# mLSTM outputs: mask sums, weights times queries and pooled remainders move from GpSimd to VectorE

## The chip, the cores and the metric

One core of one Trainium2 chip. The metric is the device time of one execution in microseconds (us), the median of 3 runs. TensorE (PE) multiplies, VectorE (DVE), ScalarE (ACT) and GpSimd (POOL) do elementwise work, SyncE (SP) issues transfers; ScalarE issues some too.

## The reference

One block of a diffusion transformer on 2048 tokens of width 1024, with 256 context tokens, in float32. The input is normalised and modulated, projected by `w_in` to a pooled half (512), queries and keys (256 each, with a short convolution and silu), values (512), an output gate o (512) and 16 gate rows. The middle is an mLSTM with 4 heads (64 wide for queries and keys, 128 for values) in both directions, beside a windowed mean of the pooled half. Then:

```python
    s = jnp.einsum('bhjd,bhsd->bhjs', qc, kc) * jnp.exp(dmat - m[..., None])
    w_inter = jnp.exp(inter - m)
    num = jnp.einsum('bhjs,bhsv->bhjv', s, vc) + w_inter[..., None] * jnp.einsum('bhvd,bhjd->bhjv', c0, qc)
    den = jnp.sum(s, axis=-1) + w_inter * jnp.einsum('bhd,bhjd->bhj', n0, qc)
    h = num / jnp.maximum(jnp.abs(den), jnp.exp(-m))[..., None]
    ...
    hn = hm * lax.rsqrt(jnp.mean(hm * hm, axis=-1, keepdims=True) + EPS)      # mlstm_output
    ...
    mix_x = jnp.concatenate([pool_x, mlstm_output(hx_m, ox, head_norm[l])], axis=-1) @ w_out[l]
    x = x + g1 * mix_x
    x = x + g2 * swiglu(modulate(rmsnorm(x, norm2[l]), sh2, sc2), w_up[l], w_down[l])
```

and a last rmsnorm. `dmat` is masked: only earlier tokens (for the other direction, later ones) count.

## The kernel before

The kernel runs in stages. To about 475 us it forms modulation, context, the projections (block products in seven instead of eight parts, `unit`) and the states of the mLSTM at the edges of 16 chunks of 128 tokens; `w_out` is loaded, scaled and split until about 515. From 505 to 820 us the outputs are formed chunk by chunk (chunks 7 to 0, then 15 to 8), and after that the up and down products of the swiglu run to the end.

Float32 products with full precision are made of three: an operand is split into a rounded part (`mh`, by ScalarE) and a remainder (`mlo`, by `split`, L151), and high times high, high times low and low times high are summed (L1171 to L1173).

The loop over chunks (from L1200) has five parts in an iteration t. `ml_a` of chunk t+1 loads a row of decay sums into X (named `raw` in the trace, 1024 wide, from `s_R`, broadcast to 128 partitions, one of three buffers), queries `qd` and a row of weights `wb` (from `s_W`, one of two buffers); TensorE forms keys times queries (`pqk`, L1090, one PSUM bank); X gets the mask added (L1092), `wb` is multiplied with the queries (L1093), ScalarE takes eight exponentials of X (L1097), and VectorE multiplies X by `pqk` (L1099). `proj` of chunk t-2 multiplies the mixed chunk by `w_out` in 48 matmuls (two halves of 24), adds the residual (L1176), stores it (`s_x`) and scales it by its norm (L1184, with the power `xrs` by GpSimd at L143). `second_norm`, in every second iteration, turns two chunks (transposes L290), applies the modulation (L297, L299), makes block sums (L306) and stores 1.8 MB to `s_hb`. `ml_b` of chunk t makes the outputs of both directions (`po`, L1114 with X, L1120 with `wb`), their divisors `rr` (L1125 to L1127), the sum of directions (L1131, L1132) and the norm of each head (L141, the power `hrs` at L143 by GpSimd, L1136). `prep` of chunk t-1 loads the gate `so`, the pooled half `pmx` and the residual, splits `pmx` (L1152), turns the head outputs (transposes L1155), gates them (L1157) and splits that (`mlo<-so`).

Three things set the order. Each engine runs its queue in the order written, and an instruction that waits holds all behind it. That order isn't the program's: a scheduler puts the instructions of each engine in order by a timeline of its own before the program is built, so that a change of engine for one instruction moves others. And buffers bind: a load of `raw` for chunk t+3 starts when the outputs of chunk t have read their X, and PSUM has three banks for projections and turns together. `ml_a` runs far ahead of its `ml_b` in this order, up to three chunks.

Of the kernel before, what the change touches and what calls it, by code (L numbers as in the profile page):

```python
# [12 lines left out]
ALU = mybir.AluOpType  # L13
# [8 lines left out]
def tile_hybrid_block(ctx: ExitStack, tc: tile.TileContext, x, c, cx, c_ctx, w_ada, b_ada, norm1, w_in, conv_qk,  # L22
                      gate_bias, pool_w, pool_scale, head_norm, w_out, norm2, w_up, w_down, norm_f, out):
    nc = tc.nc
    P = 128
# [20 lines left out]
    def r32(ap):  # L46
        return ap.bitcast(F32)
# [98 lines left out]
    def split(src, hi, lo, eng_hi, eng_lo):  # L146
        if eng_hi is nc.scalar:
            nc.scalar.copy(hi, src)  # L148
        else:
            eng_hi.tensor_copy(hi, src)  # L150
        eng_lo.tensor_tensor(lo, src, r32(hi), op=ALU.subtract)  # L151
# [207 lines left out]
    with pool("adap", 4, "right") as ap_:  # L359
        xc, turned = None, None  # L360
        for g in range(4):
            ks = range(2 * g, 2 * g + 2)
            pm = tp.tile([P, 512], F32, name="tp")[0:4, :]
# [37 lines left out]
            def col(o):  # L401
# [3 lines left out]
                                    op=ALU.add)  # L405
# [432 lines left out]
    for half in range(2):  # L838
# [8 lines left out]
        if half == 0:  # L847
# [11 lines left out]
            with pool("gp", 1) as gp:  # L859
# [5 lines left out]
                mask = gat.rearrange("p c g -> p (c g)").rearrange("p (d j) -> p d j", d=2)  # L865
# [29 lines left out]
    def dma_kv(kp, sk, sv, cc, bufs, vp=None):  # L895
        kT = kp.tile([P, 2, P], F32, name="kT", bufs=bufs)
        nc.sync.dma_start(kT, sk[:, cc * P:(cc + 1) * P].rearrange("(t p) c -> p t c", p=P))
        vt = vp.tile([P, 4, 129], F32, name="vta", bufs=2) if vp else vtp.tile([P, 4, 129], F32, name="vt")
        nc.sync.dma_start(vt.rearrange("p h v -> p (h v)"), sv[cc * P:(cc + 1) * P, :])
        return kT, vt  # L900
# [170 lines left out]
    def ml_a(n, cc):  # L1071
        csl = slice(cc * P, (cc + 1) * P)
        kT, vt = dma_kv(m2, s_k, s_v, cc, 2)
        qb = qbd[n % 2]
        qd = ld2.tile([P, 4, P], F32, name="qd")
        sq_ = s_q[:, csl]
        for hh in range(2):
            hs = slice(hh * 64, hh * 64 + 64)
            nc.sync.dma_start(qb[hs, :, hh, :], sq_.rearrange("(a b p) c -> b p a c", a=2, b=2)[hh])
            nc.sync.dma_start(qd[hs], sq_.rearrange("(h p) c -> p h c", p=64))  # L1080
        X = rwp.tile([P, 2, 4, P], F32, name="raw")
        nc.sync.dma_start(X.rearrange("p d h j -> p (d h j)"),
                          s_R[cc:cc + 1].rearrange("o d h j -> o (d h j)").to_broadcast([P, 8 * P]))
        wb = ld2.tile([P, 4, P], F32, name="wb")
        for d in range(2):
            ml_last[0] = nc.sync.dma_start(wb[d * 64:d * 64 + 64].rearrange("p h j -> p (h j)"),
                              s_W[cc, d:d + 1].rearrange("o h j -> o (h j)").to_broadcast([64, 4 * P]))
        pqk = pqp.tile([P, 512], F32, name="pqk")
        for p_ in range(2):
            nc.tensor.matmul(pqk[:, p_ * 256:(p_ + 1) * 256], lhsT=kT[:, p_, :],  # L1090
                             rhs=qb[:, p_].rearrange("p h c -> p (h c)"), start=True, stop=True)
        nc.gpsimd.tensor_tensor(X, X, mask[:, :, None, :].to_broadcast([P, 2, 4, P]), op=ALU.add)  # L1092
        nc.gpsimd.tensor_tensor(wb, wb, qd, op=ALU.mult)  # L1093
        with tc.issue_after(last_act[0].ins), tc.issue_after((copies[-1] if n else last_act[0]).ins):
            for d in range(2):
                for h in range(4):
                    nc.scalar.activation(X[:, d, h, :], X[:, d, h, :], AF.Exp, bias=tokq[:, 0, d, h, cc:cc + 1])  # L1097
        Xd = X.rearrange("p d h j -> p d (h j)")
        ml_last[1] = nc.vector.tensor_tensor(Xd, Xd, pqk[:, None, :].to_broadcast([P, 2, 512]), op=ALU.mult)  # L1099
        return X, wb, vt  # L1100
# [38 lines left out]
    def prep(cc, hm):  # L1139
        csl = slice(cc * P, (cc + 1) * P)  # L1140
        so = ld2.tile([P, 4, P], F32, name="so")
        with tc.issue_after(copies[-4].ins):
            nc.scalar.dma_start(so, s_so[:, csl].rearrange("(h p) c -> p h c", p=P))
        pm = ld2.tile([P, 4, P], F32, name="pmx")
        with tc.issue_after(copies[-4].ins):
            nc.scalar.dma_start(pm, s_pm[:, csl].rearrange("(h p) c -> p h c", p=P))
        xt = xl.tile([P, D], F32, name="big")
        with tc.issue_after(copies[-4].ins):
            nc.scalar.dma_start(xt, x[csl, :])
        mh = wk2.tile([P, 8, P], F32R, name="mh")  # L1150
        mlo = wk2.tile([P, 8, P], F32R, name="mlo")
        split(pm, mh[:, 0:4], mlo[:, 0:4], nc.scalar, nc.vector if cc == order[0] else nc.gpsimd)  # L1152
        ptr = pmp.tile([P, 512], F32, name="pm")
        for h in range(4):
            nc.tensor.transpose(out=ptr[:, h * P:(h + 1) * P], in_=hm[:, h, :], identity=ident)  # L1155
        sof = so.rearrange("p h c -> p (h c)")
        nc.vector.tensor_tensor(sof, ptr, sof, op=ALU.mult)  # L1157
        split(so, mh[:, 4:8], mlo[:, 4:8], nc.scalar, nc.vector)
        return xt, mh, mlo
# [37 lines left out]

    order = [NCH // 2 - 1 - i for i in range(NCH // 2)] + [NCH - 1 - i for i in range(NCH // 2)]
    A_, H_, M_, X_ = {0: ml_a(0, order[0])}, {}, {}, {}
    for t in range(NCH + 2):  # L1200
        if t + 1 < NCH:
            A_[t + 1] = ml_a(t + 1, order[t + 1])
# [17 lines left out]
        if 0 <= m < NCH:  # L1220
            M_[m] = prep(order[m], H_.pop(m))
# [344 lines left out]
```

## Time and profile before

| | us |
|---|---|
| median of 3 runs | 2119.07 |
| lowest, highest | 2118.11, 2120.87 |
| profiled execution | 2117.76 |
| its span (first to last instruction) | 2115.9 |
| TensorE busy | 2015.6 (95%) |
| VectorE busy | 1365.8 (65%) |
| ScalarE busy | 899.1 (42%) |
| GpSimd busy | 227.0 (11%) |

The chain that ended last is TensorE for 74% of the span, DMA for 11%, VectorE for 5%, ScalarE for 4% and GpSimd for 1%. The shares are means over stages with different limits; the stage of the change is about 300 of the 2116 us, and it is read by itself below. "Idle before" in a row is the time in which the engine stood still just ahead of that instruction, with what ended it.

### The profile page before, as it was taken

What the parts mean: (1) busy time and instruction counts of PE and PEld (TensorE: products, weight loads), DVE (VectorE), ACT (ScalarE), POOL (GpSimd) and SP (SyncE); (2) the same over time, 40 slices, a digit from 0 to 9 for tenths busy, and PEclk for the clock granted to TensorE, in tenths of its full rate; (3) what the DMA queues carried; (4) which work ended last, traced back from release to release, by engine and by line L of the source; (5) the groups of instructions that cost most, each with busy time, mean ns of one, the idle gap of its engine ahead of it and who ended that gap; (6) DMA issues with size and microseconds to landing.
All of it is one profiled execution on the core that took longest, in us unless ns stands there. A gap on an engine that the chain in (4) does not pass through costs nothing.

```text
span 2115.9 us, 27589 instructions
## 1 busy us (share of the span) xinstructions
PE 2015.6 (95%) x9482; PEld 1637.0 (77%) x9482; DVE 1365.8 (65%) x2333; ACT 899.1 (42%) x1787; POOL 227.0 (11%) x222
## 2 busy tenths in 40 slices
PE   7999989996999998999999999999999999999998
PEld 3997757775777776788888877888888788888887
DVE  6866868757455566666675588677677554447664
ACT  6643644456444444433333354333333343433442
POOL 1000013211333320000000000000000002004121
PEclk9999999997999999999999999999999999999999
DMA  8598989689586756433342367555565584644642
GB/s 281 169 297 270 301 269 329 219 262 254 138 253 209 241 184 183 140 124 125 100 159 85 100 217 256 189 194 189 174 199 192 190 309 149 226 139 168 226 158 100
DMA packets 365812, 421.42 MB, mean 199 GB/s; under 512 B 23924, under 2 KB 241624, under 8 KB 364904
## 3 DMA queue, kind: packets, MB, share of 16 engines
q1 hardware_dynamic: 319728, 348.22, 50.9%
q10 hardware_dynamic: 45944, 71.43, 10.5%
q8 instruction: 75, 1.23, 0.2%
q14 instruction: 65, 0.53, 0.1%
HBM read 280.45 MB, written 139.12 MB: 198 GB/s over the span
## 4 chain that ended last, share of the span: by engine, by line
PE 74%; DMA 11%; DVE 5%; ACT 4%; issue 3%; SPq 1%; POOL 1%; ACTq 0%; DVEq 0%; POOLq 0%
PE pa L642 8%; PE pa L644 8%; PE pa L643 8%; PE pdn L1392 7%; PE pdn L1393 7%; PE pdn L1394 7%; PE pg L642 4%; PE pg L643 4%; PE pg L644 4%; PE pb L642 2%; PE pb L644 2%; PE pb L643 2%; PE pm L1171 2%; PE pm L1173 2%; PE pm L1172 2%
## 5 line engine op out<-in xcount | busy, mean ns | idle before, releaser
L642 PE MATMUL pa<-h,wh 128*128 128x512 f32 x680 | 271.0, 400 | 7.6 <-ACT p L656 4.7
L644 PE MATMUL pa<-h,wl 128*128 128x512 f32 x680 | 269.8, 397 | 0.3 <-DMA wl<-s_w 0.3
L643 PE MATMUL pa<-h,wh 128*128 128x512 f32 x680 | 269.5, 397 | 0.0
L148 ACT CAST wh<-ws 128x512 fp32r<-128x512 f32 x200 | 123.5, 619 | 281.3 <-PE pg L643 154.2
L1392 PE MATMUL pdn<-ow,op 128*128 128x512 f32 x616 | 236.8, 389 | 1.0 <-ACT op L148 1.0
L1393 PE MATMUL pdn<-ow,op 128*128 128x512 f32 x616 | 237.5, 389 | 0.0
L1394 PE MATMUL pdn<-ow,op 128*128 128x512 f32 x616 | 237.5, 389 | 0.0
L151 DVE TENSOR_TENSOR op<-ra,op 128x512 fp32r<-128x512 f32 x154 | 121.6, 796 | 159.4 <-ACT op L148 159.3
L148 ACT CAST op<-ra 128x512 fp32r<-128x512 f32 x154 | 95.2, 621 | 225.9 <-PE pdn L1394 223.9
L642 PE MATMUL pg<-h,wh 128*128 128x512 f32 x448 | 177.8, 397 | 2.9 <-ACT h L148 1.7
L643 PE MATMUL pg<-h,wh 128*128 128x512 f32 x448 | 178.6, 399 | 0.9 <-DVE h L151 0.8
L644 PE MATMUL pg<-h,wl 128*128 128x512 f32 x448 | 177.5, 396 | 0.0
L151 DVE TENSOR_TENSOR wl<-ws,wh 128x512 fp32r<-128x512 f32 x200 | 136.4, 685 | 55.4 <-ACT wh L148 55.2
L642 PEld LDWEIGHTS pa<-h,wh 128*128 128x128 f32 x680 | 129.0, 190 | 43.2 <-ACT p L656 6.0
L644 PEld LDWEIGHTS pa<-h,wl 128*128 128x128 f32 x680 | 128.5, 189 | 31.1 <-issue 0.5
L643 PEld LDWEIGHTS pa<-h,wh 128*128 128x128 f32 x680 | 128.8, 189 | 30.2 <-issue 1.0
L1424 POOL TENSOR_TENSOR hr<-hr,o 128x1024 f32<-128x1024 f32 x8 | 21.7, 2734 | 1096.7 <-ACT o L1437 927.0
L1392 PEld LDWEIGHTS pdn<-ow,op 128*128 128x128 f32 x616 | 115.6, 188 | 25.5 <-ACT op L148 1.4
L1393 PEld LDWEIGHTS pdn<-ow,op 128*128 128x128 f32 x616 | 115.7, 188 | 23.9
L1394 PEld LDWEIGHTS pdn<-ow,op 128*128 128x128 f32 x616 | 115.7, 188 | 23.9
L613 DVE TENSOR_TENSOR ws<-raw 128x512 f32<-128x512 f32 x100 | 69.0, 690 | 96.3 <-DMA raw<-in_w_up_dram 92.0
L148 ACT CAST vt<-raw 128x512 fp32r<-128x512 f32 x112 | 69.2, 619 | 96.0 <-PE pb L643 41.2
(357 smaller groups left out, 4330.5 us busy)
## 6 DMA issues: line engine op xcount, KB each, us to landing
raw<-in_w_up_dram SPq DMA_DIRECT2D x88, 512.0 KB
ra<-s_act SPq DMA_DIRECT2D x66, 512.0 KB
s_act<-adaw SPq DMA_DIRECT2D x84, 256.0 KB
rwt<-s_t SPq DMA_DIRECT2D x77, 256.0 KB
adaw<-in_w_ada_dram SPq DMA_DIRECT2D x64, 256.0 KB
s_act<-g SPq DMA_DIRECT2D x63, 256.0 KB
s_hb<-hb SPq DMA_DIRECT2D x7, 1792.0 KB
hst<-s_hb ACTq DMA_DIRECT2D x48, 256.0 KB
```

The source lines that it names most:

```text
L148: nc.scalar.copy(hi, src)
L151: eng_lo.tensor_tensor(lo, src, r32(hi), op=ALU.subtract)
L613: nc.vector.tensor_tensor(t, a, b, op=op)
L642: nc.tensor.matmul(ps, lhsT=ah[:, k], rhs=B[:, 0, k], start=st, stop=False, **kw)
L643: nc.tensor.matmul(ps, lhsT=ah[:, k], rhs=B[:, 1, k], start=False, stop=False, **kw)
L644: mm_last[0] = nc.tensor.matmul(ps, lhsT=al[:, k], rhs=B[:, 0, k], start=False, stop=(k == 3), **kw)
L1171: nc.tensor.matmul(pt, lhsT=mh[:, k], rhs=w[:, 0, k % 4], start=(k == 0), stop=False)
L1172: nc.tensor.matmul(pt, lhsT=mh[:, k], rhs=w[:, 1, k % 4], start=False, stop=False)
L1173: nc.tensor.matmul(pt, lhsT=mlo[:, k], rhs=w[:, 0, k % 4], start=False, stop=(k == 7))
L1392: nc.tensor.matmul(ps, lhsT=A[:, 0, ts_], rhs=W[:, 0], start=start, stop=False)
L1393: nc.tensor.matmul(ps, lhsT=A[:, 0, ts_], rhs=W[:, 1], start=False, stop=False)
L1394: nc.tensor.matmul(ps, lhsT=A[:, 1, ts_], rhs=W[:, 0], start=False, stop=stop)
```

## The change

Three lines change the engine of one operation each: the sum of X and mask, the product of weights and queries, and the remainder of the pooled half (which the first chunk already had on VectorE).

```diff
--- before.py
+++ after.py
@@ -1089,8 +1089,8 @@
         for p_ in range(2):
             nc.tensor.matmul(pqk[:, p_ * 256:(p_ + 1) * 256], lhsT=kT[:, p_, :],
                              rhs=qb[:, p_].rearrange("p h c -> p (h c)"), start=True, stop=True)
-        nc.gpsimd.tensor_tensor(X, X, mask[:, :, None, :].to_broadcast([P, 2, 4, P]), op=ALU.add)
-        nc.gpsimd.tensor_tensor(wb, wb, qd, op=ALU.mult)
+        nc.vector.tensor_tensor(X, X, mask[:, :, None, :].to_broadcast([P, 2, 4, P]), op=ALU.add)
+        nc.vector.tensor_tensor(wb, wb, qd, op=ALU.mult)
         with tc.issue_after(last_act[0].ins), tc.issue_after((copies[-1] if n else last_act[0]).ins):
             for d in range(2):
                 for h in range(4):
@@ -1149,7 +1149,7 @@
             nc.scalar.dma_start(xt, x[csl, :])
         mh = wk2.tile([P, 8, P], F32R, name="mh")
         mlo = wk2.tile([P, 8, P], F32R, name="mlo")
-        split(pm, mh[:, 0:4], mlo[:, 0:4], nc.scalar, nc.vector if cc == order[0] else nc.gpsimd)
+        split(pm, mh[:, 0:4], mlo[:, 0:4], nc.scalar, nc.vector)
         ptr = pmp.tile([P, 512], F32, name="pm")
         for h in range(4):
             nc.tensor.transpose(out=ptr[:, h * P:(h + 1) * P], in_=hm[:, h, :], identity=ident)
```

The scheduler then orders every engine anew. On GpSimd only the powers of L143 are left in the loop over chunks. On VectorE 16 sums, 16 products and 15 remainders come in. Three places:

VectorE, the outputs of the third chunk, from the divisors `rr` on, before:

```order
L1125 SCALAR_TENSOR_TENSOR rr<-po,tokq 128x8
L1126 TENSOR_TENSOR rr<-po,rr 128x8
L1157 TENSOR_TENSOR so<-pm,so 128x512
L1127 RECIPROCAL rr<-rr 128x8
L151 TENSOR_TENSOR mlo<-so,mh 128x512
L1132 SCALAR_TENSOR_TENSOR h_4459<-po,rr,hf 128x128 x2
L1176 TENSOR_TENSOR big<-pm,big 128x512
L1099 TENSOR_TENSOR raw<-raw,pqk 128x1024
```

and after the change:

```order
L1125 SCALAR_TENSOR_TENSOR rr<-po,tokq 128x8
L1126 TENSOR_TENSOR rr<-po,rr 128x8
L1157 TENSOR_TENSOR so<-pm,so 128x512
L1127 RECIPROCAL rr<-rr 128x8
L1092 TENSOR_TENSOR raw<-raw,gat 128x1024
L151 TENSOR_TENSOR mlo<-so,mh 128x512
L1132 SCALAR_TENSOR_TENSOR h_4459<-po,rr,hf 128x128
L1093 TENSOR_TENSOR wb<-wb,qd 128x512
L1099 TENSOR_TENSOR raw<-raw,pqk 128x1024
```

The sum (of a chunk further on) stands directly ahead of the remainder `mlo<-so`, and the product stands between the sums of directions. The outputs of the second, fourth and sixth chunk have the sum ahead of that remainder too; in the others it stands behind.

VectorE near the end of the loads of keys and of the last convolution, before:

```order
L741 TENSOR_TENSOR pre_4131<-pa,p_4372 128x512
L151 TENSOR_TENSOR wl<-raw,wh 128x512
L948 TENSOR_TENSOR kw<-pb,wkc 128x512
L948 TENSOR_TENSOR kw<-gps,tokq 128x512
L472 SCALAR_TENSOR_TENSOR y<-pre_4131,vecs,y 128x1025
L473 SCALAR_TENSOR_TENSOR y<-pre_4131,vecs,y 128x1025
```

and after:

```order
L741 TENSOR_TENSOR pre_4131<-pa,p_4372 128x512
L151 TENSOR_TENSOR wl<-raw,wh 128x512
L1092 TENSOR_TENSOR raw<-raw,gat 128x1024
L948 TENSOR_TENSOR kw<-pb,wkc 128x512
L472 SCALAR_TENSOR_TENSOR y<-pre_4131,vecs,y 128x1025
L1092 TENSOR_TENSOR raw<-raw,gat 128x1024
L473 SCALAR_TENSOR_TENSOR y<-pre_4131,vecs,y 128x1025
```

The first two sums come in here, the second between the two steps of the convolution (`y`).

VectorE behind the projection that the outputs of the ninth chunk run beside, before:

```order
L1099 TENSOR_TENSOR raw<-raw,pqk 128x1024
L141 TENSOR_SCALAR hms<-s_6515 128x4
L1176 TENSOR_TENSOR big<-pm,big 128x512
L1136 TENSOR_TENSOR h_4459<-h_4459,hrs 128x512
L141 TENSOR_SCALAR xms<-s_6632 128x1
L1125 SCALAR_TENSOR_TENSOR rr<-po,tokq 128x8
```

and after:

```order
L1099 TENSOR_TENSOR raw<-raw,pqk 128x1024
L141 TENSOR_SCALAR hms<-s_6515 128x4
L1093 TENSOR_TENSOR wb<-wb,qd 128x512
L1176 TENSOR_TENSOR big<-pm,big 128x512
L151 TENSOR_TENSOR mlo<-pmx,mh 128x512
L1136 TENSOR_TENSOR h_4459<-h_4459,hrs 128x512
L141 TENSOR_SCALAR xms<-s_6632 128x1
L1125 SCALAR_TENSOR_TENSOR rr<-po,tokq 128x8
```

The product and the remainder now stand ahead of L1136, which the transposes L1155 need.

## Rows read from the trace of the kernel before

**Rows 1.** Windows: us, busy us (x instructions) of each engine, granted clock, DMA share, GB/s
```profile
460.00:540.00 80.00, 55.02 (x274) 45.02 (x273) 53.56 (x115) 44.39 (x117) 11.36 (x8) 0.81 0.82 228
540.00:800.00 260.00, 241.27 (x1353) 197.80 (x1353) 142.50 (x291) 118.02 (x367) 85.16 (x68) 0.98 0.68 202
```

**Rows 2.** Waits of TensorE, 540 to 800: total us, times, longest us
```profile
PE pm L290 <- DVE big L1184: 7.2, 3, 3.4
PE pm L1155 <- DVE rr L1125: 3.8, 2, 2.2
PE pm L1173 <- DVE mlo L151: 2.5, 2, 1.7
...
PE pqk L1090 <- PE pm L1173: 1.4, 2, 0.9
```

**Rows 3.** Groups by line, GpSimd, 400 to 840: busy us, mean ns | idle before
```profile
L1092 POOL TENSOR_TENSOR raw<-raw,gat 128x1024 f32<-128x1024 f32 x16 | 39.1, 2445 | 87.8 <-DMA raw<-s_R 56.5 <-DVE h L151 17.0 <-issue 6.9
L1093 POOL TENSOR_TENSOR wb<-wb,qd 128x512 f32<-128x512 f32 x16 | 20.8, 1297 | 67.6 <-DMA wb<-s_W 44.1 <-DMA qd<-s_q 8.7 <-DMA kT<-s_k 7.9
L151 POOL TENSOR_TENSOR mlo<-pmx,mh 128x512 fp32r<-128x512 f32 x15 | 19.2, 1278 | 38.1 <-ACT mh L148 25.9 <-PE pm L290 8.0 <-PE pm L1173 3.3
```

**Rows 4.** Groups by line, VectorE, 540 to 800
```profile
L1099 DVE TENSOR_TENSOR raw<-raw,pqk 128x1024 f32<-128x1024 f32 x12 | 14.6, 1217 | 8.9 <-ACT raw L1097 5.2 <-PE pm L1173 3.4 <-issue 0.3
L151 DVE TENSOR_TENSOR mlo<-so,mh 128x512 fp32r<-128x512 f32 x14 | 13.2, 941 | 3.8 <-ACT mh L148 3.8
...
L1184 DVE TENSOR_SCALAR big<-big,xrs 128x1024 f32<-128x1024 f32 x14 | 11.5, 825 | 25.7 <-DMA s_x<-big 17.7 <-POOL xrs L143 7.9
```

**Rows 5.** Timeline, third chunk's outputs: start us, us, instruction [idle before <-releaser]
```profile
549.80 0.33 SPq L1082 DMA_DIRECT2D raw<-s_R  x1
...
552.82 0.69 DVE L151 TENSOR_TENSOR mlo<-so,mh 128x512 fp32r<-128x512 f32 x1 [0.58 <-ACT mh L148]
...
554.35 2.40 POOL L1092 TENSOR_TENSOR raw<-raw,gat 128x1024 f32<-128x1024 f32 x1 [6.17 <-DMA raw<-s_R]
...
554.98 0.39 PE L1173 MATMUL pm<-h,mlo 128*128 128x512 f32 x1
```

**Rows 6.** Timeline, TensorE where it waited, 527 to 715
```profile
527.47 0.79 PE L1090 MATMUL pqk<-h,kT 128*128 128x256 f32 x1 [6.56 <-DVE raw L1099]
...
602.87 0.63 PE L1155 MATMUL pm<-ident,h 128*128 128x128 f32 x4 [1.63 <-DVE rr L1125]
...
608.87 0.51 PE L1173 MATMUL pm<-h,mlo 128*128 128x512 f32 x1 [1.69 <-DVE mlo L151]
...
645.21 1.61 PE L290 MATMUL pm<-ident,big 128*128 128x128 f32 x8 [3.41 <-DVE big L1184]
...
714.09 1.09 PE L1155 MATMUL pm<-ident,h 128*128 128x128 f32 x4 [2.17 <-DVE rr L1125]
```

**Rows 7.** Timeline, GpSimd and VectorE, 598 to 607
```profile
598.67 1.29 POOL L1093 TENSOR_TENSOR wb<-wb,qd 128x512 f32<-128x512 f32 x1 [5.79 <-DMA kT<-s_k]
...
605.90 2.37 POOL L1092 TENSOR_TENSOR raw<-raw,gat 128x1024 f32<-128x1024 f32 x1 [2.49 <-DMA raw<-s_R]
...
606.44 2.38 DVE L151 TENSOR_TENSOR mlo<-so,mh 128x512 fp32r<-128x512 f32 x1 [0.21 <-ACT mh L148]
```

**Rows 8.** Timeline, a late product's row and the slowest sum's row
```profile
675.50 1.27 POOL L1093 TENSOR_TENSOR wb<-wb,qd 128x512 f32<-128x512 f32 x1 [1.01 <-DMA wb<-s_W]
...
676.40 0.60 PE L1155 MATMUL pm<-ident,h 128*128 128x128 f32 x4
...
733.28 2.70 SPq L1082 DMA_DIRECT2D raw<-s_R  x1
...
743.33 2.41 POOL L1092 TENSOR_TENSOR raw<-raw,gat 128x1024 f32<-128x1024 f32 x1 [7.06 <-DMA raw<-s_R]
```

**Rows 9.** Timeline, last convolution of queries, 429 to 432
```profile
429.38 1.29 DVE L473 SCALAR_TENSOR_TENSOR y<-pre,vecs,y 128x1025 f32<-128x1025 f32 x1
...
431.76 2.38 POOL L1092 TENSOR_TENSOR raw<-raw,gat 128x1024 f32<-128x1024 f32 x1 [6.88 <-issue]
```

## The prediction

> **What bounds the kernel now.** I read the windows first, because the change touches only the stretch in which the mLSTM outputs are formed. From 540 to 800 us TensorE is busy 241.27 of 260 us at a granted clock of 0.98, VectorE 142.50 and GpSimd 85.16 [rows 1]. So TensorE bounds this stretch, and all that can be gained in it is its 18.7 idle us. From 460 to 540 TensorE is busy only 55.02 of 80 us at a granted clock of 0.81: there the chain runs through loads of w_out and the first exponentials, and what GpSimd does may lie in it.
>
> The view of waits says next what TensorE's idle time between 540 and 800 was spent on [rows 2]: 7.2 us for normalised rows (L1184), 3.8 for the root-mean-square chain (named rr, but see below), 2.5 for the remainders mlo, 1.4 at the products of keys and queries. The three groups that move hold 39.1, 20.8 and 19.2 us of GpSimd [rows 3], 79 us altogether, but over half of the idle time before the first two ended at a DMA: GpSimd spends this stage waiting for rows to land. That is what I weigh most. GpSimd is in order, and so is VectorE: the wait moves with the instruction.
>
> **What is removed.** On GpSimd one sum takes 2445 ns, one product 1297, one remainder 1278 [rows 3]. VectorE does 128x1024 of such an operation in 1217 ns (L1099) [rows 4] and 128x512 in 0.69 us [rows 5]. So VectorE gets 16 x 1.22 + 31 x 0.69 = 40.9 us more in all, about 2.6 per chunk, and at 142.5 of 260 us busy it has room for them. The gains, stall by stall:
>
> - Contention. The remainder of the second half, mlo<-so, takes 0.69 us alone [rows 5] and took 2.38 us while GpSimd's sum ran from 605.90 to 608.27 [rows 7]; TensorE then waited 1.69 us at L1173 [rows 6]. Its mean is 941 ns over 14 [rows 4], so others were stretched too. With no tensor work left on GpSimd I take back all 2.5 us of this wait [rows 2].
> - Hidden queueing on GpSimd. The transposes L1155 wait 1.63 us at 602.87 and 2.17 us at 714.09 [rows 6]. The releaser printed is rr, but rr is done early; the one that is late is L1136, which needs the power hrs, and hrs stands on GpSimd behind a product L1093 that waited for its row (start 598.67 in the first case [rows 7]). VectorE does the product in 0.69 instead of 1.29 us, and hrs no longer stands behind it; the wait for the row stays. I take 2.6 of the 3.8 us.
> - The 3.41 us at 645.21 [rows 6]: TensorE waited for L1184, which needs the power xrs from GpSimd's queue, and the store of the same rows. Of L1184's idle time 17.7 us ended at that store and only 7.9 at the power [rows 4], so I take 0.7, between 0 and 3.41.
> - The products of keys and queries wait for a free bank, that is for L1099, which waits for the exponentials, which wait for the sum. 1.4 us in this stretch [rows 2]: all of it. At 527.47 the same chain costs 6.56 us [rows 6]; the sum is 1.2 us shorter, so I take 1.3 there.
>
> Together 2.5 + 2.6 + 0.7 + 1.4 + 1.3 = 8.5 us.
>
> **What is added.** The order on VectorE decides it. In four of the outputs (of the second, third, fourth and sixth chunk) the sum now stands directly ahead of mlo<-so, for which TensorE waits within the same projection. In the third chunk the load of the sum's row was issued at 549.80, the row was there at 554.35 (start of the sum), and the remainder ran at 552.82 because it was queued elsewhere; TensorE needed it at 554.98 [rows 5]. In the new order VectorE stands at the sum until 554.35, then 1.22 + 0.69: the remainder is ready at 556.26, 1.3 us late. I take that for each of the four: 5.2 us. The bounds: nothing if the row lands 1.3 us sooner, and where it lands as late as the slowest one, 10.05 us after its issue (733.28 to 743.33) [rows 8], 4 x (10.05 - 4.55 + 1.3) = 27.2.
>
> The product waits for rows too. At 675.50 it started 0.90 us before L1155 at 676.40 [rows 8]; on VectorE there now stand behind it half of a residual sum, a remainder and L1136, which L1155 needs: 675.50 + 4 x 0.65 = 678.1, 1.7 us late. Bounds 0 and the two L1155 waits again, 3.8.
>
> Near 430 us the second sum now stands between the two steps of the last convolution. Its row is there at 431.76, and L473 started at 429.38 [rows 9]. L473 would start at 431.76 + 1.22 = 432.98, 3.6 us late, and with it the scalar engine's activation, the store of queries, and the weight loads behind that store on the sync queue. Operands are made ahead, so I take 1.0 of 0 to 3.6.
>
> Last, 2.6 us more VectorE per chunk delay what is in line behind them: L1184 ahead of the second norm's transposes, and evacuations of banks. The waits that could grow are the 7.2 us of [rows 2]; bounds 0 and, were none of it beside TensorE's work, 40.9. I take 2.0, near the lower end, as VectorE is idle 45% of the stretch.
>
> Losses: 5.2 + 1.7 + 1.0 + 2.0 = 9.9. Net +1.4 us. The profiled execution took 2117.76 us (span 2115.9 and 1.9 around it), so 2119.2 by its measure; the median of the three runs is 1.3 above it, hence 2120.5, which I round to 2120: about no change.
>
> **Rivals.** Slower: the landing of the row decides. One mechanism: VectorE stands at L1092 while mlo<-so is behind it. For the remainder to be in time in the third chunk, the sum must start by 554.98 - 0.69 - 1.22 = 553.07, 3.3 us after the issue; each us beyond it costs TensorE one in every chunk so ordered. At 4.55 us it is my 1.3; halfway to the slowest, at 7.3 us, it is 4.05 in each of four chunks, 16.2 in place of 5.2, and the time is 2131. For it: most of GpSimd's idle time before the sum was such a wait, 56.5 of 87.8 us [rows 3]. Against it: in the other chunks the sum stands behind the remainder.
>
> Faster: the waits vanish and the new ones stay hidden, as the row lands before VectorE comes to it, or the projection's matmuls that need no remainder cover it. Then the gains stay, with the 3.41 us whole: 8.5 + 2.7 = 11.2, less some 2 for the convolution and the product: 2117.8 - 9.2 + 1.3 = 2110. For it: the stretched remainder and the L1155 waits, which no order of VectorE brings back. Against it: the order, in which four chunks have the sum ahead. The Trainium skill stands on this side (Perfetto Trace Analysis, section Optimizing GPSIMD Operations): "Prefer implementations on other engines where possible." The rows agree that each of the three operations is about half as long on VectorE, but a shorter operation that has to wait is not an earlier one.
>
> A third way is that nothing changes but the engine, all being off the path: 2119. It lies inside my forecast and gets no case of its own.
>
> **How the numbers follow.** Forecast (terms about as sized, 2115 to 2124): 0.40. Slower rival, 2124 and above: 0.31. Faster rival, below 2115: 0.29. What a measurement of this kernel can tell from no change is about 0.2%, 4.2 us, that is 2114.8 and 2123.3. The forecast's own case spills 0.02 over the upper and 0.01 under the lower bound: faster 0.30, same 0.37, slower 0.33. The range must go to both rivals, 2107 to 2135; it is not symmetric because the bound of the landings, 27.2, is larger than that of the gains.
>
> **What would show it.** Right: in the new profile GpSimd holds only powers in the stretch; mlo<-so is at 0.69 each time; L1092 on VectorE takes 1.22 with idle time before it that ends at the load of raw, and TensorE waits 1 to 2 us at L1173 behind it in some chunks; the waits for L1155 fall below 2 us. Wrong: TensorE's idle time from 540 to 800 below 12 us (then the new waits are hidden) or above 28 (then the landings decide), or a change outside 420 to 820 us larger than 3 us, which no step here provides for.

## The result and the profile after

The changed kernel took 2133.47 us (median of 4 runs, 2131.68 to 2141.54), the kernel before 2119.44 (4 runs, 2118.11 to 2120.87). The ratio is 1.0070 with a 95% interval of 1.0053 to 1.0087: slower by 14 us. The profiled execution took 2131.68 us, span 2129.9, against 2117.76 and 2115.9. The forecast was 2120 and about no change, and so was missed by 13 us; the range ended at 2135, and the rival on the slow side gave 2131.

Windows of both kernels, cut at the same work instead of the same time: up to the first outputs (L1114), from there to the last transposes of the second norm (L290), and the rest. Columns as in [rows 1]. First the kernel before:

```profile
0.00:508.80 508.80, 454.29 (x2406) 367.42 (x2407) 361.64 (x693) 266.54 (x482) 72.93 (x120) 0.95 0.84 265
508.80:823.50 314.70, 283.11 (x1554) 231.49 (x1553) 175.91 (x364) 138.86 (x426) 94.97 (x74) 0.96 0.68 202
823.50:2115.90 1292.40, 1278.18 (x5525) 1038.08 (x5523) 828.23 (x1279) 493.74 (x883) 59.12 (x28) 1.00 0.51 172
```

and after the change:

```profile
0.00:509.90 509.90, 453.34 (x2406) 365.33 (x2407) 363.38 (x698) 267.09 (x483) 61.26 (x115) 0.96 0.84 264
509.90:835.60 325.70, 288.30 (x1554) 232.99 (x1553) 196.76 (x407) 138.69 (x424) 27.31 (x32) 0.94 0.65 196
835.60:2129.90 1294.30, 1279.37 (x5525) 1038.76 (x5523) 825.81 (x1278) 492.72 (x882) 59.95 (x28) 1.00 0.52 172
```

Of the 14 us, 11.0 are in the stage of the outputs, with the same 1554 matmuls. TensorE's idle time there grew from 31.6 to 37.4 us, by 5.8, and its busy time from 283.1 to 288.3, by 5.2: the same matmuls ran longer, at a mean granted clock of 0.94 instead of 0.96. An estimate from windows of 4 us (busy time, times one less the granted clock) puts 8.9 us down to the lower clock before and 13.4 after, 4.4 of the 5.2. So nearly half of the loss stands in no row of waits. VectorE is busy 60% of the stretch.

TensorE's waits between 540 and 800 us (us in total, times, longest us), against [rows 2]:

```profile
PE pm L1173 <- DVE mlo L151: 6.9, 5, 2.8
PE pm L290 <- DVE hb L297: 5.3, 2, 2.7
PE pm L290 <- DVE so L1157: 2.3, 3, 1.3
PE pm L1155 <- DVE h L1136: 2.1, 3, 0.9
PE pm L290 <- DVE big L1184: 2.0, 3, 1.5
```

What was to go went in part: L1155 waits 2.1 instead of 3.8 us, L1184 2.0 instead of 7.2, and the wait at the products of keys and queries is gone. The wait for the remainder mlo<-so rose from 2.5 to 6.9, and the one of L290 for evacuations (L297, which empty a PSUM bank) to 5.3 us. In the kernel before the latter was:

```profile
PE pm L290 <- DVE hb L297: 1.8, 1, 1.8
```

The window holds the same time of both kernels, not the same work. The groups on VectorE, 400 to 840 us (busy us, mean ns, idle time before, with what ended it), against [rows 3]:

```profile
L1092 DVE TENSOR_TENSOR raw<-raw,gat 128x1024 f32<-128x1024 f32 x16 | 19.6, 1224 | 21.0 <-DMA raw<-s_R 21.0
L1093 DVE TENSOR_TENSOR wb<-wb,qd 128x512 f32<-128x512 f32 x16 | 11.0, 688 | 10.9 <-DMA wb<-s_W 8.5 <-DMA kT<-s_k 2.4
L151 DVE TENSOR_TENSOR mlo<-so,mh 128x512 fp32r<-128x512 f32 x16 | 10.9, 684 | 1.9 <-ACT mh L148 1.9
```

The sums and products are as short as worked out, 1224 and 688 ns, and no remainder is stretched any more: 684 ns instead of 909 over the same 16 (941 over the 14 in [rows 4]). But VectorE now stands still for 31.9 us ahead of them, until a load has landed. One such place, in the outputs of the fourth chunk (timeline; start us, us, instruction, idle before and releaser):

```profile
566.67 0.33 SPq L1082 DMA_DIRECT2D raw<-s_R  x1
...
573.11 1.23 DVE L1092 TENSOR_TENSOR raw<-raw,gat 128x1024 f32<-128x1024 f32 x1 [3.69 <-DMA raw<-s_R]
574.25 0.68 DVE L151 TENSOR_TENSOR mlo<-so,mh 128x512 fp32r<-128x512 f32 x1
...
574.99 0.80 PE L1173 MATMUL pm<-h,mlo 128*128 128x512 f32 x1 [2.57 <-DVE mlo L151]
```

The row landed 6.4 us after its issue, VectorE waited 3.69 us at the sum with the remainder behind it, and TensorE 2.57 us for the remainder. What followed stands in the windows around it:

```profile
570.00:574.00 4.00, 2.42 (x15) 1.76 (x13) 0.89 (x1) 0.22 (x1) 0.00 (x0) 1.00 0.51 156
574.00:578.00 4.00, 3.01 (x7) 2.44 (x8) 2.94 (x6) 3.63 (x13) 0.00 (x0) 0.59 0.33 98
578.00:582.00 4.00, 4.00 (x20) 3.28 (x20) 3.58 (x9) 2.15 (x9) 0.00 (x0) 0.98 0.25 72
```

After TensorE had stood still the granted clock was 0.59 over four microseconds, of its two levels mostly the lower (1.2 GHz), and TensorE did 7 matmuls there, against 20 in the next four. From the end of the wait, 574.99, to 578.00 the granted clock was 0.50 throughout, and matmuls of L1171 to L1173 started 0.43 us apart instead of 0.23. A wait of 2.6 us was thus followed by 3.0 us of slow matmuls, which by these numbers cost an estimated 1.5 us more. Elsewhere it was 0.53 and 0.50 from 612 to 620, where three waits of 1.49, 1.28 and 2.82 us followed on each other, and 0.70 from 696 to 700, behind the wait shown next. The second mechanism is seen around 695 us, VectorE and TensorE:

```profile
691.61 1.23 DVE L1092 TENSOR_TENSOR raw<-raw,gat 128x1024 f32<-128x1024 f32 x1 [1.64 <-DMA raw<-s_R]
692.75 0.35 DVE L1132 SCALAR_TENSOR_TENSOR h<-po,rr,hf 128x128 f32<-128x128 f32 x1
693.98 0.69 DVE L1093 TENSOR_TENSOR wb<-wb,qd 128x512 f32<-128x512 f32 x1 [0.89 <-DMA kT<-s_k]
694.65 0.55 DVE L297 TENSOR_SCALAR hb<-pm,A,B 128x256 f32<-128x256 f32 x1
```

```profile
695.25 0.66 PE L290 MATMUL pm<-ident,big 128*128 128x128 f32 x4 [2.63 <-DVE hb L297]
```

Here no remainder was behind the wait but the evacuation of a bank (L297), and the next transposes had no bank for 2.63 us.

### The profile page after: what moved, and what is told of

It reads as the page before. It is cut to its first block, busy times and chain, and to the rows that moved or that the text cites. A ratio compares the mean times of both kernels' runs of the same rounds, so it can differ in the third digit from the quotient of the medians.

```text
span 2129.9 us, 27513 instructions
## 1 busy us (share of the span) xinstructions
PE 2021.0 (95%) x9482; PEld 1637.1 (77%) x9482; DVE 1385.9 (65%) x2380; ACT 898.5 (42%) x1787; POOL 148.5 (7%) x175
## 4 chain that ended last, share of the span: by engine, by line
PE 73%; DMA 14%; DVE 5%; ACT 3%; issue 2%; SPq 2%; ACTq 0%; POOL 0%; DVEq 0%; POOLq 0%
PE pa L642 8%; PE pa L644 8%; PE pa L643 8%; PE pdn L1392 7%; PE pdn L1393 7%; PE pdn L1394 7%; PE pg L642 4%; PE pg L644 4%; PE pg L643 4%; DMA wb<-s_W 2%; PE pb L642 2%; PE pb L644 2%; PE pb L643 2%; PE pm L1173 2%; PE pm L1171 2%
## 5 line engine op out<-in xcount | busy, mean ns | idle before, releaser
L644 PE MATMUL pa<-h,wl 128*128 128x512 f32 x680 | 270.1, 398 | 1.5 <-DMA wl<-s_w 1.5
L644 PE MATMUL pg<-h,wl 128*128 128x512 f32 x448 | 177.6, 397 | 0.1
L644 PEld LDWEIGHTS pa<-h,wl 128*128 128x128 f32 x680 | 128.8, 189 | 32.7 <-DMA wl<-s_w 1.9
L1171 PE MATMUL pm<-h,mh 128*128 128x512 f32 x256 | 107.1, 418 | 3.9 <-ACT mh L148 1.7
L1173 PE MATMUL pm<-h,mlo 128*128 128x512 f32 x256 | 103.3, 410 | 7.1 <-DVE mlo L151 6.9
```

Source lines behind the costliest of these rows:

```text
L644: mm_last[0] = nc.tensor.matmul(ps, lhsT=al[:, k], rhs=B[:, 0, k], start=False, stop=(k == 3), **kw)
L1171: nc.tensor.matmul(pt, lhsT=mh[:, k], rhs=w[:, 0, k % 4], start=(k == 0), stop=False)
L1173: nc.tensor.matmul(pt, lhsT=mlo[:, k], rhs=w[:, 0, k % 4], start=False, stop=(k == 7))
```

## Experiments

Two theories stood against each other. A: VectorE, in order, stands at a sum or product until its row has landed, and what TensorE needs stands behind it. B: VectorE simply has 41 us more to do, and its chains grow by that, waits or not. Ratios are to the kernel before, measured in the same round of runs on the same chip.

**One edit at a time.** Each puts the other two operations back on GpSimd. For the sum alone:

```diff
+        nc.vector.tensor_tensor(X, X, mask[:, :, None, :].to_broadcast([P, 2, 4, P]), op=ALU.add)
         nc.gpsimd.tensor_tensor(wb, wb, qd, op=ALU.mult)
...
         split(pm, mh[:, 0:4], mlo[:, 0:4], nc.scalar, nc.vector if cc == order[0] else nc.gpsimd)
```

> 

> Only the sum of X and mask is on VectorE; product and pooled remainder stay on GpSimd. Theory A (landings: VectorE stands at the sum until its row is there, and what TensorE needs stands behind it): most of the 14 us stays, 2127 to 2134, with TensorE waits at L1173 for mlo of 4 us or more between 540 and 800. Theory B (load: 41 us more VectorE work lengthen its chains, whatever waits): about half of the work is added, so half of the loss, 2126, with no large wait at L1173.

Measured: 2129.90 us, ratio 1.0053 (1.0036 to 1.0070). L1173 waited 5.1 us for mlo, and VectorE idled 28.5 us ahead of the sum:

```profile
PE pm L1173 <- DVE mlo L151: 5.1, 3, 2.4
L1092 DVE TENSOR_TENSOR raw<-raw,gat 128x1024 f32<-128x1024 f32 x16 | 19.5, 1222 | 28.5 <-DMA raw<-s_R 28.5
```

That fits A; by the time alone, within B's reach too.

> 

> Only the product of weights and queries is on VectorE. A: its row is late in few chunks and other work stands between, so 2117 to 2123. B: a quarter of the added work, +3.7, so 2123. In both GpSimd still stretches mlo<-so where its sum runs beside it.

Measured: 2125.62 us, ratio 1.0048 (1.0032 to 1.0064). More than A or B gave: a miss of both. VectorE's row (400 to 840) and TensorE's waits between 540 and 800, from the slowest of its nine executions (2136.55 us, 10.9 above the median, so these waits may be larger than in most):

```profile
L1093 DVE TENSOR_TENSOR wb<-wb,qd 128x512 f32<-128x512 f32 x16 | 14.1, 879 | 32.1 <-DMA wb<-s_W 32.1
```

```profile
PE pm L290 <- DVE big L1184: 10.0, 5, 3.3
PE pm L290 <- DVE hb L297: 5.9, 2, 3.7
PE pm L1171 <- DVE hb L297: 3.4, 2, 2.6
```

The product's row is late far more often than the expectation took it to be, and [rows 3] had it: 44.1 us of GpSimd's idle time before the product ended at the load of wb. Here 32.1 us of VectorE's time went to it, 9.3 us of TensorE's to evacuations and 10.0 to normalised rows (L1184). VectorE's 32.1 us ended at a load, and are not work. The expectation was wrong on mlo<-so too: its mean was 685 ns, not stretched, with the sum still on GpSimd, because none started while an operation ran there.

> 

> Only the pooled remainder is on VectorE; it waits for no landing row of the mLSTM. A: no loss, 2114 to 2119. B: a quarter of the added work, +3.5, so 2122.5.

Measured: 2121.52 us, ratio 1.0019 (0.9999 to 1.0039). This operation waits for no late row. The time lies above A's range and beside B's figure, but the interval takes in nothing and 0.4%: a small cost can't be told from none. The largest wait of TensorE in its trace, 10.6 us at L1171 for ScalarE's `mh`, is one that neither theory names. The three single edits add up to 1.2%, more than the 0.70% of the change, so the loss can't be shared out among them.

**The same work, in another order.** `split` returns its last instruction, `prep` keeps it in a list `rem_`, and the sum is queued behind it:

```diff
-        nc.vector.tensor_tensor(X, X, mask[:, :, None, :].to_broadcast([P, 2, 4, P]), op=ALU.add)
+        with tc.issue_after((rem_[n - 4] if n >= 4 else last_act[0]).ins): nc.vector.tensor_tensor(X, X, mask[:, :, None, :].to_broadcast([P, 2, 4, P]), op=ALU.add)
...
+        rem_.append(split(so, mh[:, 4:8], mlo[:, 4:8], nc.scalar, nc.vector))
```

> 

> All three on VectorE as in the change, but the sum of chunk n is kept behind the remainder mlo<-so of chunk n-4, in all chunks. A: the waits at L1173 for mlo (6.9 us between 540 and 800) fall below 1.5, and with them the stretches of half clock behind them, so 2120 to 2127; what stays is work behind the sum and the product other than that remainder. B: VectorE does the same work, so 2131 to 2135.

Measured: 2118.85 us, ratio 1.0001 (0.9988 to 1.0014). All of the loss is gone, with all three operations still on VectorE; A had left 1 to 8 us of it, B all. VectorE's row (400 to 840), the window 540 to 800 and TensorE's largest waits in it:

```profile
L1092 DVE TENSOR_TENSOR raw<-raw,gat 128x1024 f32<-128x1024 f32 x16 | 19.6, 1222 | 10.7 <-DMA raw<-s_R 10.6
540.00:800.00 260.00, 244.13 (x1367) 199.07 (x1366) 164.91 (x334) 119.53 (x371) 24.15 (x30) 0.99 0.67 204
PE pm L1171 <- ACT mh L148: 3.6, 2, 3.4
PE pm L290 <- DVE big L1184: 3.4, 5, 1.1
PE pm L290 <- DVE hb L297: 3.2, 2, 2.6
```

No wait at L1173 for mlo is left; VectorE's idle time at the sum is 10.7 us instead of 21.0. VectorE is busier here (164.91 us) than in the change (158.57), which B can't explain. The same edit with only the sum on VectorE:

> 

> As e1 (only the sum on VectorE), but the sum of chunk n behind mlo<-so of chunk n-4, product and pooled remainder on GpSimd. A: the loss of e1 (0.5%) goes with the order: 2112 to 2120, with L1173 waiting less than 2 us for mlo between 540 and 800. If the sum's engine itself costs the time: 2126 to 2130 as e1.

Measured: 2115.83 us, ratio 1.0000 (0.9985 to 1.0014), against 1.0053 for the sum alone without it. The pair has the same operations on the same engines; what differs is the order asked for, and what the scheduler made of it on the other engines.

**The product behind, too.** `nrm_` holds the instructions of L1136:

```diff
+        with tc.issue_after((nrm_[n - 2] if n >= 2 else last_act[0]).ins): nc.vector.tensor_tensor(wb, wb, qd, op=ALU.mult)
```

> 

> As e4 (the sum of chunk n behind mlo<-so of chunk n-4), and the product of chunk n kept behind L1136, the norm of the heads of chunk n-2. Theory A (what stands behind a waiting sum or product decides): VectorE's idle time at the product falls below 4 us (e4: 8.8), TensorE's idle between 540 and 800 stays at 16 us or below, time 2112 to 2118, at or below e4. Theory B (VectorE's added work): no change from e4 or, the work being the same, 2118 to 2122.

Measured: 2124.14 us, ratio 1.0038 (1.0016 to 1.0060): a miss, above both ranges. The idle time at the product did fall, to 2.0 us, but VectorE came to the sum sooner and waited there 19.3 us instead of 10.7, with evacuations behind it. TensorE's waits, 540 to 800:

```profile
PE pm L290 <- DVE hb L297: 5.3, 3, 2.6
PE pm L1171 <- DVE hb L297: 4.6, 2, 3.6
PE pm L290 <- DVE big L1184: 3.0, 4, 1.2
```

The longest stands at one sum: VectorE waited 4.23 us for the row until 648.73, two evacuations (L297) stood behind it, and TensorE waited 3.61 us until 650.72. Idle time taken out at the product came back at the sum (19.5 us for the two in the run before, 21.3 here). This kernel was then given twice the added work, on a scratch tile, without a row to wait for:

```diff
+        with tc.issue_after(rem_[-1].ins): [nc.vector.tensor_tensor(misc[:, 3592:4096], misc[:, 3592:4096], misc[:, 3592:4096], op=ALU.add) for _ in range(4)]
```

> 

> As e5, with four more VectorE sums of 128x504 per chunk on a scratch tile (64 in all, their result unused), about 2.7 us per chunk, behind mlo<-so: VectorE's added work is doubled, and no landing row is waited for. A: within 4 us of e5. B (the work itself lengthens VectorE's chains): 10 us or more above e5.

Measured: 2124.16 us, ratio 1.0039 (1.0023 to 1.0055), the same as without. VectorE's busy time between 540 and 800, before and with the work:

```profile
540.00:800.00 260.00, 239.54 (x1336) 195.59 (x1335) 162.23 (x329) 117.06 (x368) 23.40 (x28) 0.97 0.69 203
```

```profile
540.00:800.00 260.00, 239.25 (x1338) 195.28 (x1338) 193.92 (x388) 117.71 (x368) 24.64 (x29) 0.98 0.69 203
```

31.7 us more on VectorE, 75% busy, and TensorE's 239 us stay. B's 10 us or more are out. That the work costs nothing at all isn't shown by this run: the scheduler's order changed with it, and VectorE's idle time at sum and product fell from 21.3 to 14.1 us, which may have paid for some of the work.

**The sum far behind.** Sum and product both behind L1136, the sum of chunk n behind that of chunk n-3:

```diff
+        with tc.issue_after((nrm_[n - 3] if n >= 3 else last_act[0]).ins): nc.vector.tensor_tensor(X, X, mask[:, :, None, :].to_broadcast([P, 2, 4, P]), op=ALU.add)
```

> 

> As e5, but the sum of chunk n is kept behind L1136 of chunk n-3 too, some 10 us after its row's load was issued. A: the idle time at the sum falls below 3 us (e4: 10.7); X is needed only two chunks later, so 2110 to 2118. It would be slower, 2120 to 2126, if the exponentials now come late for the one bank of keys times queries: then waits at L1090 grow above 3 us between 540 and 800.

Measured: 2115.21 us, ratio 0.9996 (0.9980 to 1.0011). The sum's idle time is 2.8 us, as expected, and no wait at the evacuations is left, but L1184 costs 10.7 us. The waits at L1090 did grow, to 3.2 us, the sign named for a slower time, and the time was not longer. With the pooled remainder back on GpSimd:

> 

> As e6 (sum and product on VectorE, both behind L1136), with the pooled remainder back on GpSimd. If what stands behind waits is all that matters, the remainder's engine costs nothing either way: 2110 to 2118, ratio to the kernel before 0.997 to 1.000. If the remainder beside VectorE's work costs (port shared by the two engines: mlo<-so, L1136 and others above their 0.69 us): 2118 to 2122.

Measured: 2110.82 us (10 runs, 2107.38 to 2115.38), ratio 0.9972 (0.9960 to 0.9984): of the ten versions the only one whose interval lies below the kernel before. Its rows on VectorE, 400 to 860, and TensorE's waits, 540 to 800:

```profile
L1092 DVE TENSOR_TENSOR raw<-raw,gat 128x1024 f32<-128x1024 f32 x16 | 20.6, 1286 | 3.3 <-DMA raw<-s_R 3.3
L1136 DVE TENSOR_TENSOR h<-h,hrs 128x512 f32<-128x512 f32 x16 | 13.1, 819 | 11.8 <-POOL hrs L143 11.8
L1093 DVE TENSOR_TENSOR wb<-wb,qd 128x512 f32<-128x512 f32 x16 | 12.0, 751 | 0.0
```

```profile
PE pqk L1090 <- issue: 6.5, 3, 3.6
PE pm L290 <- DVE big L1184: 5.0, 5, 3.9
PE pm L1171 <- ACT mh L148: 3.0, 3, 2.5
PE pm L1171 <- DVE big L1176: 2.3, 2, 1.8
```

VectorE stands still for 3.3 us at sums and products together, where the change had 31.9. Beside a remainder on GpSimd VectorE's operations are longer again (1286, 819 and 751 ns, against 1219, 691 and 684 in the version with all three on VectorE), and the time is not: the second expectation, 2118 to 2122, is out. And with product and remainder on GpSimd:

> 

> Only the sum on VectorE, kept behind L1136 of chunk n-3; product and remainder on GpSimd. The last candidate to beat the kernel before. Theory A: VectorE's idle time at the sum below 3 us (e8: 13.4), GpSimd no longer late with powers because of the sum, so 2108 to 2116, ratio 0.995 to 0.999. Against it: hrs may still stand behind the product on GpSimd, and the waits at L1155 (6.4 us in e8) stay; then the ratio is 1.000.

Measured: 2114.09 us, ratio 0.9990 (0.9977 to 1.0004); the sum's idle time was 3.1 us, the waits at L1155 0.5, the mean of mlo<-so 747 ns. The median fits A, but the interval reaches to no gain at all.

## Why the prediction came out as it did

**The mechanism was in it, on the rival's side.** "VectorE stands at L1092 while mlo<-so is behind it" is what the trace shows and what the pairs with the sum behind the remainder undid. I gave the rival 0.31 and the forecast 0.40, and the forecast of no change was wrong. That the time came within 3 us of the rival's 2131 is in part luck: its 16.2 us of waits for the remainder were 5.9 in the four chunks that it names, and evacuations and the clock made up the rest.

**The waits for the remainder**, taken as 4 x 1.3 = 5.2 us, came to 5.9 in the four chunks with the sum ahead (6.9 with two more). The size was near by luck: in the second, third, fourth and sixth chunk the sum started 4.2, 3.9, 6.4 and 8.3 us after the issue, and TensorE waited too little to be listed, 0.48, 2.57 and 2.82. I took the nearest row, 4.55, for all four, though the eleven rows loaded between 540 and 800 us in the kernel before were used 4.5 to 10.05 us after their issue, with a median of 6.15. After the change the median of the nine for which VectorE waited there was 7.1, near the rival's 7.3; but two of its four chunks were among the early ones, and the 9.7 us beyond its 3.3 cost 5.9, not one us each.

**What else stands behind a wait** was the larger miss, and with the clock the step that failed. Under "What is added" I named what was queued behind the sum in four chunks and behind the product in one, and put evacuations into a term of 2.0 us. The evacuations (L297) cost 5.3 us instead of the 1.8 before, at chunks where the sum stands behind the remainder and so seemed harmless. Moving the product alone lost 0.5% without a late sum on VectorE.

**The clock was not in the sum at all.** Every term was a wait. The stage lost 5.8 us to idle time and 5.2 to longer matmuls; in the windows around 574 us the granted clock fell behind the wait. My test of the rival, more than 28 us idle between 540 and 800, failed in part for that reason: it was 22.1 (260 less 237.86), against 18.7, and the time still rose by 14. A window of fixed time also leaves out what the longer stage pushes behind its end: it held 1308 matmuls after the change and 1353 before.

**The gains** were nearly right: the contention is gone (684 ns), L1155 gave 1.7 of the 2.6 us taken, the products of keys and queries their 1.4, and L1184 gave more, 5.2 where 0.7 was taken. The 527 us wait, 6.56, is 6.13: 0.4 instead of 1.3. **The convolution**, taken as 1.0 us, shows no cost: L473 started at 435.83 behind a sum that waited 2.85 us, 6.4 us later than before, but between 440 and 460 TensorE was busy all 20 us in both kernels. Its wait at L644 for weights, 1.50 us (0.28 before), ended at 430.57, ahead of that sum. **The added work**, 2.0 us, can't be told from nothing in the run with 31.7 us more; what the term was also to cover, the evacuations, is the miss above.

**The rule of the Trainium skill** (Perfetto Trace Analysis, section Optimizing GPSIMD Operations), to prefer other engines, holds for each instruction here: half as long on VectorE. The kernel didn't follow it: with all three moved and the waits out of the way the ratio was 0.9996, and it was below 1 only with the remainder back on GpSimd.

What stays open: whether the remainder costs something on VectorE, and why (0.9999 to 1.0039 alone; 0.9996 against 0.9972 in the far-behind pair, from two rounds of runs on two chips, with intervals that overlap); and how idle time at the sum turns into time, since the order with only the sum kept behind (e4, 19.5 us idle at sum and product) cost nothing and that with both (e5, 21.3) 0.4%: what stood behind differed, but that was read from the traces and not tried by itself. A fourth buffer for the row, which might let it land earlier in the same order, was not tried.

## What to carry to other kernels

Before moving an operation to another in-order engine, look at what it waits for: if it is a landing transfer, the wait moves with it, and the cost is what stands behind it in the new queue, at every place and not only at the worst one. Put such an instruction behind the work that TensorE needs next, as late as its own consumer allows; here the order alone turned +0.7% into no loss, and with one operation back on GpSimd the kernel was 0.3% faster than before. Price a stall of TensorE at more than its length, because the matmuls after it may run at the lower clock.

## What the runs showed of the hardware

- A sum on GpSimd stretched a two-input operation of VectorE on 128x512 from 0.69 to 2.38 us; without tensor work on GpSimd the mean over 16 fell from 909 to 684 ns. With only the product or only the pooled remainder moved, and the sum still on GpSimd, it was 685 and 687. In the kernel before, the three stretched ones of the 16 (606.44, 680.67, 755.48) started while an operation on GpSimd ran; in those two versions none did.
- A row broadcast to 128 partitions (512 KB) was used by the sum that waited for it 3.9 to 10.05 us after its issue, in the same stage of the two kernels.
- Behind a TensorE wait of 2.57 us the granted clock was 0.50 for 3.0 us (0.59 over 574 to 578), and 0.98 over 578 to 582.
- 31.7 us more work on VectorE in 260, to 75% busy, left the time as it was (1.0039 against 1.0038), while VectorE's idle time at sum and product fell by 7.2 us.
